# Two of the four sums of weight blocks per unit of seven products, formed by accumulating DMA transfers in place of VectorE additions

## The chip, the cores and the metric

One Trainium2 chip, one of its cores. The engines are TensorE (PE, matrix products), VectorE (DVE), ScalarE (ACT), GpSimd (POOL) and SyncE (SP, which here only issues DMA transfers); PEld are TensorE's weight loads. The metric is the device time of one execution in microseconds, lower is better. Before the change: median 2028.73 us of 3 runs (2027.09 to 2028.84).

## What is computed

Three blocks one after the other on 512 rows of width 1024, all in float32: a block with three mixers (pooling, stick-breaking attention, attention to a memory) and a gated FFN; a block with a gated recurrence and an FFN; a block with latent attention and an FFN. The change touches the three FFNs. The reference, cut to these:

```python
# first block (D_FF = 2816)
gu = n2 @ w_ffn_in[l]                                   # 1024 x 5632
ff = (jax.nn.silu(gu[..., :D_FF]) * gu[..., D_FF:]) @ w_ffn_out[l]

# second and third block
def _conv_ffn(h, w_up, conv_w, conv_b, w_down):
    u = h @ w_up                                        # 1024 x 5632
    ...
    gate, up = jnp.split(y, 2, axis=-1)                 # y: u after a causal convolution over 3 rows
    return (jax.nn.silu(gate) * up) @ w_down
```

## The kernel before, in words

**Products.** Every float32 operand is split into a high part (a copy rounded by ACT, `split`, line 113) and a low part (VectorE subtracts the copy from the original, line 114). A product is three matmuls: high x high, high x low, low x high (`mm3`, lines 107 to 110).

**The FFN.** `ffn` (line 935) goes over the 22 column blocks of 128 in steps of two (line 1007). The first step is done by another routine (`projA_first`). In the ten others, the gate half of the weights is a *unit of seven products*, `seven` (line 304). In the first FFN (`conv is None`) the up half is a unit too, so it has 20 units; the other two FFNs have 10 each, and their up half is an ordinary projection (`projA`, 48 matmuls over 512 columns, with two weight loads of 512 KB). There are 40 units in the program.

**A unit** forms 256 output columns by a scheme of the Strassen kind, with seven half-size products where the ordinary way has eight. The weights of two column blocks, A[0] and A[1], each come as one raw tile of 1024 x 128 (512 KB); each is seen as two halves, A[i][0] and A[i][1] (256 KB each, 128 partitions x 4 runs of 128 numbers). Four sums of these quarter blocks are formed on VectorE (`usum`, lines 324 to 328):

- u1 = A[1][0] + A[1][1], line 333, into a tile of its own (tag "u", two copies)
- u3 = A[0][0] + A[1][0], line 335, in place of A[1][0]
- u2 = u3 + A[1][1], line 336, into a second tile of tag "u"
- u4 = u2 + A[0][1], line 349, in place of u2

The seven products, in order, take as weights A[0][0], u1, u2, A[0][1], u3, A[1][1], u4. `product` (line 317) splits the weights into a tile of tag "w" (eight copies, so that splits can run ahead of TensorE) and issues 12 matmuls over 256 columns. They accumulate in three areas of two PSUM banks: pY, pX, pZ. pX holds the second product, is read by VectorE's subtraction (line 344, which calls line 68), and only then may the seventh product be added to it.

The sums of the activations that the units need (nT1, T3, nT2, T4) are formed once for each FFN by `x_sums` (line 281), on VectorE, in the profile the rows FT<-FT and xc<-FT.

**Buffers and queues.** A[0]'s raw tile lies in the pool wp, A[1]'s in the FFN's own pool; each has two copies. All loads are issued by SyncE (`load`, line 76), in order; a load waits until the last reader of the tile copy that it overwrites is done. The last reader of A[1] is the split of the sixth product (A[1][1]). `seven` is a generator: between its `yield`s, the caller interleaves the units, so that the first product of a unit comes ahead of products six and seven of the one before:

```python
g7 = gate7(f)
next(g7)          # loads, first product
run(tail)         # products 6 and 7 of the unit before
next(g7)          # products 2 to 5
```

**The order of instructions** on each engine is not that of the text: the framework's scheduler orders them by its own estimate of when each is ready, and places semaphores for what depends on what. An engine executes its instructions in that order.

GpSimd executes the powers of the norms (`rstd_of`, line 125), ahead of each FFN's units, and issues no DMA.

**Names in the profile.** Buffer numbers are left out, and the output tile of an up unit of the first FFN is also called u. u1 and u2 are both "u<-raw" (u3 lies in A[1]'s raw tile); u3 is "raw<-raw,raw"; u4 is "u<-u,raw"; the low part of a split is "wu<-raw,wu" or "wu<-u,wu" on DVE, its high part "wu<-raw" or "wu<-u" on ACT.

Of the kernel before, what the change touches and what calls it, by code (L numbers as in the profile page):

```python
# [10 lines left out]
F32 = mybir.dt.float32  # L11
# [4 lines left out]
ALU = mybir.AluOpType  # L16
# [3 lines left out]
P = 128  # L20
# [14 lines left out]
def kernel(ctx: ExitStack, tc: tile.TileContext, a: dict, out: bass.AP):  # L35
    nc = tc.nc
    uid = [0]

    def nm(s):
        uid[0] += 1  # L40
        return f"{s}_{uid[0]}"
# [11 lines left out]
    def bank(s, tag="pj"):  # L53

        return ps.tile([P, 512], F32, tag=tag, name=nm(s), bufs=4 if tag == "pj" else 1)
# [5 lines left out]
    def act(out_, in_, func, **kw):  # L61
        return nc.scalar.activation(out=out_, in_=in_, func=func, **kw)  # L62

    def tt(out_, in0, in1, op):
        return nc.vector.tensor_tensor(out=out_, in0=in0, in1=in1, op=op)  # L65

    def stt(out_, in0, scalar, in1, op0, op1):
        return nc.vector.scalar_tensor_tensor(
            out=out_, in0=in0, scalar=scalar, in1=in1, op0=op0, op1=op1
        )  # L70
# [5 lines left out]
    def load(dst, src):  # L76
        return nc.sync.dma_start(out=dst, in_=src)
# [29 lines left out]
    def mm3(out_, sta, mov, first, last, **kw):  # L107
        nc.tensor.matmul(out_, lhsT=sta[0], rhs=mov[0], start=first, stop=False, **kw)  # L108
        nc.tensor.matmul(out_, lhsT=sta[0], rhs=mov[1], start=False, stop=False, **kw)  # L109
        nc.tensor.matmul(out_, lhsT=sta[1], rhs=mov[0], start=False, stop=last, **kw)  # L110

    def split(src, hi, lo):
        act(hi, src, AF.Copy)
        tt(lo, src, hi.bitcast(F32), ALU.subtract)
# [189 lines left out]
    def seven(w, col, ops, xp, dst, c21, done):  # L304

        A = []
        for i in range(2):
            raw = (wp, xp)[i].tile([P, KD, P], F32, tag="raw", name=nm("raw"), bufs=2)  # L310
            load(raw, w[:, col + i * P : col + (i + 1) * P].rearrange("(k p) n -> p k n", p=P))
            A.append([raw.rearrange("p (c j) n -> p j c n", j=2)[:, j] for j in range(2)])
        bY, bXZ = bank("Y"), bank("XZ")
        pY, pX, pZ = bY[:, :256], bXZ[:, :256], bXZ[:, 256:]
        lf, rt = slice(0, 256), slice(256, 512)

        def product(o, src, key, first):
            t_ = wp.tile([P, 2, 4, P], F32R, tag="w", name=nm("wu"))
            split(src, t_[:, 0], t_[:, 1])
            x_ = ops[key]  # L320
            for c in range(4):
                mm3(o, (t_[:, 0, c], t_[:, 1, c]), (x_[0][:, c], x_[1][:, c]), first and c == 0, c == 3, skip_group_check=True)

        def usum(a_, b_, o=None):
            if o is None:
                o = xp.tile([P, 4, P], F32, tag="u", name=nm("u"), bufs=2)
            tt(o, a_, b_, ALU.add)
            return o

        product(pY, A[0][0], (0, 0), True)  # L330
        act(dst[0][:, lf], pY, AF.Copy)
        yield 1
        u1 = usum(A[1][0], A[1][1])
        product(pX, u1, "nT1", True)
        u3 = usum(A[0][0], A[1][0], A[1][0])
        u2 = usum(u3, A[1][1])
        product(pY, u2, "nT2", False)
        act(dst[0][:, rt], pY, AF.Copy)
        product(pZ, A[0][1], (1, 0), False)
        tt(dst[0][:, lf], pZ, dst[0][:, lf], ALU.add)  # L340
        done(0, 0)
        product(pY, u3, "T3", False)
        act(dst[1][:, rt], pY, AF.Copy)
        stt(dst[1][:, rt], pX, -1.0, dst[1][:, rt], ALU.mult, ALU.subtract)
        done(1, 1)
        yield 1
        product(pY, A[1][1], "T4", False)
        c21(dst[1][:, lf], pY)
        product(pX, usum(u2, A[0][1], u2), (1, 1), False)
        tt(dst[0][:, rt], pX, dst[0][:, rt], ALU.add)  # L350
        done(0, 1)
# [583 lines left out]
    def ffn(w_up, w_down, X, steps, xpool, conv, gpost, gnext, nxt, side="left"):  # L935
        FT = ff["FT"]
        with tc.tile_pool(name=nm("fx"), bufs=1, reuse_waits="tile", side=side) as E:
# [29 lines left out]
            def gate7(f):  # L967

                if conv is None:
                    dst = [FT[:, f], FT[:, f + 1]]  # L970

                    def c21(o, src):
                        act(o, src, AF.Silu, scale=-1.0)

                    def done(q, l):
                        if (q, l) == (1, 1):
                            act(dst[1][:, rt], dst[1][:, rt], AF.Silu)
                        elif (q, l) == (0, 1):
                            act(dst[0], dst[0], AF.Silu)
                else:  # L980
                    dst = [row("g7"), row("g7")]

                    def c21(o, src):
                        act(o, src, AF.Copy, scale=-1.0)
                        gate(f, 1, dst[1])

                    def done(q, l):
                        if (q, l) == (0, 1):
                            gate(f, 0, dst[0])
                return seven(w_up, f * P, ops, E, dst, c21, done)  # L990

            def up7(f):
                dst = [row("u7"), row("u7")]

                def c21(o, src):
                    stt(FT[:, f + 1, lf], src, -1.0, FT[:, f + 1, lf], ALU.mult, ALU.mult)

                def done(q, l):
                    if (q, l) == (1, 1):
                        tt(FT[:, f + 1, rt], FT[:, f + 1, rt], dst[1][:, rt], ALU.mult)  # L1000
                    elif (q, l) == (0, 1):
                        tt(FT[:, f], FT[:, f], dst[0], ALU.mult)
                return seven(w_up, DFF + f * P, ops, E, dst, c21, done)
# [484 lines left out]
```

## Time and profile before

| | |
|---|---|
| time, median of 3 runs | 2028.73 us |
| the profiled execution's own time | 2036.45 us |
| its span | 2034.6 us |
| PE / DVE / ACT / POOL busy | 1990.5 / 1277.1 / 958.0 / 56.4 us |
| DMA | 183.44 MB, 90 GB/s in the mean |
| first FFN's units | about 446 to 657 us of the span |
| second FFN's, third FFN's | about 1110 to 1320 us, 1690 to 1900 us |

The page gives for each engine its busy time, share of the span and number of instructions. The views used below are: a table of stretches (busy time of each engine between two moments); a list of waits (who waited for whom, in total us, times, the longest); the instructions of one tile (smallest/median/largest ns, and what ended the engine's idle time ahead of them); the timeline (start us, duration, engine, line, operation, out<-in; in brackets the idle time ahead of it and what ended it); the chain of work that ended last.

### The profile page before, as it was taken

The page shows a single profiled execution, that of the slowest core. Times are in us where ns is not written, and L with a number is a line of the kernel's source. Part 1 is how long each engine was busy: PE and PEld are TensorE (multiplying, and loading weights), DVE is VectorE, ACT ScalarE, POOL GpSimd, SP SyncE. Part 2 cuts the span into 40 slices and gives each one's busy share as a digit, 9 for nine tenths or more (in the row PEclk, how much of TensorE's full clock was granted, in tenths as well). Part 3 has the DMA queues.
Part 4 walks back from the last instruction along what each step waited for, and adds up shares of the span by engine and source line. Part 5 has one row for each costly group of instructions (what it writes and reads, how often), then busy time and mean ns, then how long its engine had stood idle before and what let it go on. Part 6 is the DMA issues. An engine that isn't in the chain of part 4 may idle for free.

```text
span 2034.6 us, 29719 instructions
## 1 busy us (share of the span) xinstructions
PE 1990.5 (98%) x11665; PEld 1701.7 (84%) x11665; DVE 1277.1 (63%) x2293; ACT 958.0 (47%) x1862; POOL 56.4 (3%) x84
## 2 busy tenths in 40 slices
PE   8999999999999999999999999999989999999999
PEld 6877778889999888888888888888887778888887
DVE  5664543489888336666556887853555558887632
ACT  5543452365555227333244555542357545555521
POOL 0000000000000000000010000000021000000000
PEclk9999999999999999999999999999989999999999
DMA  6332224324333332222213233332230113333322
GB/s 223 90 92 73 69 77 124 104 84 125 102 106 105 93 93 84 73 63 72 70 46 89 83 113 96 93 105 93 66 96 32 42 48 106 96 104 94 104 93 83
DMA packets 192482, 183.44 MB, mean 90 GB/s; under 512 B 6999, under 2 KB 159830, under 8 KB 192342
## 3 DMA queue, kind: packets, MB, share of 16 engines
q1 hardware_dynamic: 192342, 181.54, 29.6%
q8 instruction: 92, 1.51, 0.3%
q14 instruction: 48, 0.39, 0.1%
HBM read 179.42 MB, written 2.10 MB: 89 GB/s over the span
## 4 chain that ended last, share of the span: by engine, by line
PE 80%; DVE 9%; DMA 5%; ACT 3%; issue 2%; POOL 1%; SPq 0%; DVEq 0%; POOLq 0%; ACTq 0%
PE B L108 10%; PE B L110 10%; PE B L109 10%; PE A L108 9%; PE A L109 9%; PE A L110 8%; PE hs L1099 2%; DVE wu L65 2%; PE Y L108 2%; PE Y L109 2%; PE Y L110 2%; DMA raw<-in_w_ffn_in_dram 2%; PE XZ L108 2%; PE XZ L109 2%; PE XZ L110 2%
## 5 line engine op out<-in xcount | busy, mean ns | idle before, releaser
L65 DVE TENSOR_TENSOR wlo<-raw,whi 128x1024 fp32r<-128x1024 f32 (+2 forms) x217 | 257.2, 1187 | 343.7 <-ACT whi L62 343.3
L62 ACT ACTIVATE whi<-raw 128x1024 fp32r<-128x1024 f32 (+2 forms) x217 | 223.9, 1033 | 376.5 <-PE B L109 256.5
L108 PE MATMUL A<-XH,whi 128*128 128x512 f32 (+1 forms) x912 | 337.1, 370 | 0.2 <-ACT XH L62 0.2
L109 PE MATMUL A<-XL,whi 128*128 128x512 f32 (+1 forms) x912 | 332.4, 365 | 0.8 <-DVE XL L65 0.8
L110 PE MATMUL A<-XH,wlo 128*128 128x512 f32 (+1 forms) x912 | 331.7, 364 | 0.0
L110 PE MATMUL B<-whi,yc 128*128 128x512 f32 x528 | 208.0, 395 | 0.0
L108 PE MATMUL B<-whi,yc 128*128 128x512 f32 x528 | 207.6, 393 | 0.0
L109 PE MATMUL B<-wlo,yc 128*128 128x512 f32 x528 | 207.3, 393 | 0.0
L110 PEld LDWEIGHTS A<-XH,wlo 128*128 128x128 f32 x912 | 173.1, 190 | 29.5 <-issue 0.2
L109 PEld LDWEIGHTS A<-XL,whi 128*128 128x128 f32 x912 | 173.3, 190 | 26.4 <-DVE XL L65 1.2
L108 PEld LDWEIGHTS A<-XH,whi 128*128 128x128 f32 x912 | 172.8, 190 | 26.8 <-ACT XH L62 0.7
L108 PE MATMUL B<-whi,XH 128*128 128x512 f32 (+2 forms) x416 | 166.8, 402 | 1.3 <-ACT whi L62 1.3
L109 PE MATMUL B<-wlo,XH 128*128 128x512 f32 (+2 forms) x416 | 158.7, 382 | 1.0 <-DVE wlo L65 1.0
L110 PE MATMUL B<-whi,XL 128*128 128x512 f32 (+2 forms) x416 | 158.7, 383 | 0.0
L108 PE MATMUL Y<-xc,wu 128*128 128x256 f32 x480 | 133.8, 279 | 5.0 <-ACT g L62 3.2
L110 PE MATMUL Y<-xc,wu 128*128 128x256 f32 x480 | 133.0, 277 | 0.0
L109 PE MATMUL Y<-xc,wu 128*128 128x256 f32 x480 | 132.9, 277 | 0.0
L62 ACT ACTIVATE wu<-raw 128x512 fp32r<-128x512 f32 x160 | 98.8, 624 | 46.2 <-DMA raw<-in_ffn_w_up_dram 34.9
L62 ACT ACTIVATE wu<-u 128x512 fp32r<-128x512 f32 x120 | 74.4, 629 | 96.8 <-PE A L109 59.8
L109 PEld LDWEIGHTS B<-wlo,yc 128*128 128x128 f32 x528 | 99.3, 188 | 22.7
L110 PEld LDWEIGHTS B<-whi,yc 128*128 128x128 f32 x528 | 99.4, 188 | 21.8
L108 PEld LDWEIGHTS B<-whi,yc 128*128 128x128 f32 x528 | 99.4, 188 | 21.8 <-issue 0.4
(325 smaller groups left out, 4201.0 us busy)
## 6 DMA issues: line engine op xcount, KB each, us to landing
raw<-in_ffn_w_up_dram SPq DMA_DIRECT2D x88, 512.0 KB
raw<-in_w_ffn_in_dram SPq DMA_DIRECT2D x44, 512.0 KB
raw<-in_ffn_w_down_dram SPq DMA_DIRECT2D x44, 512.0 KB
raw<-in_w_in_dram SPq DMA_DIRECT2D x42, 512.0 KB
raw<-in_hgrn_w_in_dram SPq DMA_DIRECT2D x32, 512.0 KB
raw<-in_w_ffn_out_dram SPq DMA_DIRECT2D x22, 512.0 KB
raw<-in_w_out_dram SPq DMA_DIRECT2D x8, 512.0 KB
raw<-in_hgrn_w_out_dram SPq DMA_DIRECT2D x8, 512.0 KB
```

Source lines behind the costliest of these rows:

```text
L62: return nc.scalar.activation(out=out_, in_=in_, func=func, **kw)
L65: return nc.vector.tensor_tensor(out=out_, in0=in0, in1=in1, op=op)
L108: nc.tensor.matmul(out_, lhsT=sta[0], rhs=mov[0], start=first, stop=False, **kw)
L109: nc.tensor.matmul(out_, lhsT=sta[0], rhs=mov[1], start=False, stop=False, **kw)
L110: nc.tensor.matmul(out_, lhsT=sta[1], rhs=mov[0], start=False, stop=last, **kw)
L1099: nc.tensor.matmul(b[:, sl], lhsT=K[:, e, sl], rhs=Q[:, e, sl], start=True, stop=True)
```

## The change

u1 and u3 are no longer added on VectorE. For u1, SyncE loads A[1][0] a second time, into a tile of its own (tag "u1", two copies; it takes the place of tag "u"), and a DMA transfer issued by GpSimd adds A[1][1] to it from DRAM. For u3, a second transfer issued by GpSimd adds A[0][0] from DRAM to A[1][0] in the raw tile. u2 is written in place of u1, u4 in place of u2 as before.

```diff
             A.append([raw.rearrange("p (c j) n -> p j c n", j=2)[:, j] for j in range(2)])
+        u1 = xp.tile([P, 4, P], F32, tag="u1", name=nm("u1"), bufs=2)
+        blk = [[w[:, col + i * P : col + (i + 1) * P].rearrange("(c j p) n -> p j c n", j=2, p=P)[:, j] for j in range(2)] for i in range(2)]
+        load(u1, blk[1][0])
+        nc.gpsimd.dma_start(out=u1, in_=blk[1][1], accum_op=ALU.add)
+        u3 = A[1][0]
+        nc.gpsimd.dma_start(out=u3, in_=blk[0][0], accum_op=ALU.add)
         bY, bXZ = bank("Y"), bank("XZ")
...
-        def usum(a_, b_, o=None):
-            if o is None:
-                o = xp.tile([P, 4, P], F32, tag="u", name=nm("u"), bufs=2)
+        def usum(a_, b_, o):
             tt(o, a_, b_, ALU.add)
             return o
...
-        u1 = usum(A[1][0], A[1][1])
         product(pX, u1, "nT1", True)
-        u3 = usum(A[0][0], A[1][0], A[1][0])
-        u2 = usum(u3, A[1][1])
+        u2 = usum(u3, A[1][1], u1)
         product(pY, u2, "nT2", False)
```

## Rows read from the trace of the kernel before

**Rows 1.** Page, part 1: busy us (share of the span) x instructions

```profile
PE 1990.5 (98%) x11665; PEld 1701.7 (84%) x11665; DVE 1277.1 (63%) x2293; ACT 958.0 (47%) x1862; POOL 56.4 (3%) x84
```

**Rows 2.** Table of stretches: length, busy us by engine, granted clock, DMA share, GB/s

```profile
457.00:646.00 189.00, 183.16 (x1582) 180.89 (x1582) 167.81 (x325) 109.44 (x222) 0.00 (x0) 1.00 0.37 107
1200.00:1320.00 120.00, 120.00 (x756) 107.01 (x755) 98.09 (x149) 67.14 (x111) 0.00 (x0) 1.00 0.32 94
1120.00:1140.00 20.00, 17.13 (x134) 16.18 (x134) 19.93 (x28) 12.52 (x20) 0.00 (x0) 1.00 0.09 28
1695.00:1705.00 10.00, 6.29 (x51) 5.92 (x50) 10.00 (x16) 7.73 (x13) 0.00 (x0) 0.97 0.17 55
1703.00:1709.00 6.00, 5.88 (x37) 5.88 (x38) 5.05 (x8) 2.44 (x5) 0.00 (x0) 0.72 0.42 134
```

**Rows 3.** List of waits, PE, 430 to 660 us: total us, times, longest

```profile
PE XZ L108 <- DVE u L68: 2.3, 5, 0.7
PE XZ L108 <- DVE FT L68: 2.1, 2, 1.9
```

**Rows 4.** Instructions of tile u on DVE, 457 to 646 us

```profile
L65 DVE TENSOR_TENSOR u<-raw x38: 676/688/696, 459.4 to 637.0; 128x512 f32<-128x512 f32 x38
...
L68 DVE SCALAR_TENSOR_TENSOR u<-XZ,u x9: 411/416/420, 472.6 to 633.9; 128x256 f32<-128x256 f32 x9
...
  DMA raw<-in_w_ffn_in_dram: 13.2, 12
```

**Rows 5.** Timeline, DVE, first FFN

```profile
526.20 0.69 DVE L65 TENSOR_TENSOR wu<-raw,wu 128x512 fp32r<-128x512 f32 x1 [0.74 <-ACT wu L62]
526.99 0.69 DVE L65 TENSOR_TENSOR wu<-u,wu 128x512 fp32r<-128x512 f32 x1
...
530.88 0.69 DVE L65 TENSOR_TENSOR u<-raw 128x512 f32<-128x512 f32 x1 [1.66 <-DMA raw<-in_w_ffn_in_dram]
531.49 0.69 DVE L65 TENSOR_TENSOR wu<-u,wu 128x512 fp32r<-128x512 f32 x1
...
538.82 0.68 DVE L65 TENSOR_TENSOR wu<-u,wu 128x512 fp32r<-128x512 f32 x1
```

**Rows 6.** Timeline, ACT, first FFN

```profile
537.04 0.63 ACT L62 ACTIVATE wu<-u 128x512 fp32r<-128x512 f32 x1 [1.74 <-PE XZ L110]
```

**Rows 7.** Timeline, PE, first FFN: first matmuls of a unit's products two, five and seven

```profile
526.26 0.28 PE L108 MATMUL XZ<-xc,wu 128*128 128x256 f32 x1
...
530.35 0.28 PE L108 MATMUL Y<-xc,wu 128*128 128x256 f32 x1
...
535.30 0.38 PE L108 MATMUL XZ<-XH,wu 128*128 128x256 f32 x1 [0.71 <-DVE u L68]
```

**Rows 8.** Chain of work that ended last: start us, us, what (ten units apart)

```profile
526.91 3.87 DMA raw<-in_w_ffn_in_dram
...
626.09 3.80 DMA raw<-in_w_ffn_in_dram
```

**Rows 9.** Timeline, DVE, start of the second FFN

```profile
1115.79 0.69 DVE L65 TENSOR_TENSOR raw<-raw,raw 128x512 f32<-128x512 f32 x1 [2.16 <-DMA raw<-in_ffn_w_up_dram]
1116.40 2.35 DVE L65 TENSOR_TENSOR FT<-FT 128x1024 f32<-128x1024 f32 x2
```

**Rows 10.** Timeline, ACT, start of the second FFN

```profile
1113.07 1.20 ACT L62 ACTIVATE FT<-tr 128x512 f32<-128x512 f32 x2 [1.52 <-DVE XL L65]
```

**Rows 11.** Timeline, DVE, start of the third FFN

```profile
1684.92 0.69 DVE L65 TENSOR_TENSOR raw<-raw,raw 128x512 f32<-128x512 f32 x1 [1.26 <-DMA raw<-in_ffn_w_up_dram]
```

**Rows 12.** Timeline, SP, ACT, PE, second FFN: load, first split, first matmul

```profile
1278.06 1.59 SPq L77 DMA_DIRECT2D raw<-in_ffn_w_up_dram  x2
...
1283.68 0.63 ACT L62 ACTIVATE wu<-raw 128x512 fp32r<-128x512 f32 x1 [2.69 <-DMA raw<-in_ffn_w_up_dram]
...
1297.04 0.28 PE L108 MATMUL Y<-XH,wu 128*128 128x256 f32 x1
```

**Rows 13.** DMA queues, 541 to 646 us: packets, MB, share of 16 engines

```profile
q1 hardware_dynamic: 19264, 10.49, 34.0%
```

## The prediction

> **What bounds the kernel now.** Read the page's busy times first: TensorE is busy 98% of the span, VectorE 63%, GpSimd 3% [rows 1]. So at most some 2% can be gained anywhere, and only where TensorE waits. The next view is the table of stretches [rows 2]. The change touches the 40 units of seven products: 20 in the first FFN (span 457 to 646 us), 10 in each of the other two. In the first FFN TensorE is busy 183.16 of 189 us, so 5.84 us are open. In the middle of the second it is busy 120.00 of 120: nothing is open there. At the starts of the second and third FFN 2.87 and 3.71 us are open, and VectorE is busy 19.93 of 20 and 10.00 of 10 us: there VectorE sets the pace.
>
> What ends TensorE's waits in the first FFN is in the list of waits: 2.3 and 2.1 us end on VectorE's subtraction at line 68, the one that frees pX for the seventh product [rows 3]. Why that comes late is in the rows of tile u: VectorE stood idle 13.2 us in 12 waits ahead of these sums until a weight load landed [rows 4]. The framework's scheduler has placed the sum u1 far ahead of its use. In the timeline the split of A[1][1] (526.20 us, 0.69 long) frees the second raw buffer, the load into it starts at 526.91 and takes 3.87 us, and u1 of the unit after next starts at 530.88, after 1.66 us of idleness [rows 5, 8]. Its consumer, the ACT copy, runs only at 537.04 [rows 6]. VectorE executes in order, so everything behind u1 waits too, and TensorE loses 0.71 us at 535.30 [rows 7].
>
> **The change, part by part.** (1) Removed from VectorE: u1 and u3, two instructions of 0.69 us per unit [rows 4], 80 in all. They start about 0.61 us apart when back to back [rows 5], so 1.2 us per unit and 49 us in all leave VectorE; almost all of that is off the path. What counts is which TensorE waits they caused.
>
> First FFN: the waits at u1 go with u1. I take away the two groups that end on line 68: 2.3 + 2.1 = 4.4 us [rows 3]. The bounds: 0, if another wait takes the place; at best TensorE's own pace. 36 matmuls start between 526.26 and 530.35, 0.1136 us each [rows 7]; two units have 168, so 19.1 us, against 19.84 us between second-buffer loads two units apart, (626.09 - 526.91) / 5 [rows 8]. That is 0.74 us per pair, 6.7 us over nine pairs.
>
> Starts of the other two FFNs: here u3 (raw<-raw,raw) waits 2.16 and 1.26 us for a load, and the sums of the activations (FT<-FT) stand right behind it, starting at 1116.40 although ACT's copies that they need ran from 1113.07 for 1.20 us [rows 9 to 11]. From there VectorE is busy without a break up to TensorE's gaps. With u3 gone I take 2.2 + 1.3 = 3.5 us, less than the 2.87 and 3.71 us that TensorE idles there [rows 2]. u3's own 0.6 us I don't count, because u2 loses its early place: it now overwrites u1 and so follows the split of u1, with one ACT copy more in series.
>
> Middle of the second and third FFN: 0. TensorE has no gap [rows 2]. The cover is the lead of the splits: ACT's copy for a first product starts at 1283.68 and that product runs at 1297.04, 13.4 us later [rows 12]. Later sums would eat from that first.
>
> (2) Added on SyncE: one 256 KB load per unit, queued behind the two raw loads and ahead of the next unit's. It waits until the seventh split of the unit two before has read the buffer: 526.99 + 0.69 = 527.68, 0.8 us after the second raw load is issued [rows 5, 8]. What stands behind it on SyncE are loads that wait for later releases, so the wait costs nothing by itself.
>
> (3) Added on GpSimd's queue: two accumulating transfers per unit. No row has one. GpSimd runs no instruction in these stretches [rows 2], so their waits hold up only each other; the norm's power steps ahead of the first unit are the exception, with one transfer each at three starts as the bound, and 0 taken. The nearest row for the price is a plain 512 KB load, 3.87 us [rows 8]. Bounds for one: half of it, 1.9 us (256 KB), and two of it, 7.7 us (both operands read, slowly). I take 3.9 us for the first, which reads as many bytes as that load, and 1.9 more for the second, whose landing can overlap: nothing orders the two.
>
> Does that hide? The second raw load and the u1 load land by 526.91 + 3.9 + 1.9 = 532.7; the first accumulation by 536.6. The ACT copy of u1 runs at 537.04 [rows 6]: just in time. u3 is there at 538.5; u2 cannot start before the split of u1 on VectorE at 538.82 is over [rows 5]. Being a little late is covered too: the seventh split of a unit is done at 527.68 and TensorE starts on that product at 535.30 [rows 5, 7], a lead of 7.6 us.
>
> (4) The DMA engines. In the first FFN the load queue takes 34.0% of their time [rows 13] for 1 MB per unit; 0.75 MB are added, 1.25 MB with the destination read. So 60 to 77%: no bound on the mean, but bursts meet (second rival).
>
> The Trainium skill alone has a price for a transfer issued by GpSimd (DMA: Bandwidth & Descriptors, section Anatomy of one DMA — SWDGE (gpsimd) path): a fit of 2.0 us plus size over 436 GB/s, an estimate of 2.6 us for 256 KB, by which the sum would be the same with more room; no run here shows it.
>
> **Sum:** -4.4 - 2.2 - 1.3 = -7.9 us. Durations are of the profiled execution (2036.45 us, span 2034.6), which is 7.7 us above the median of 2028.73; I carry the difference over: 2020.8, so 2021 us.
>
> **Rivals.** *The accumulations bound the first FFN (slower).* The second raw buffer has two copies, so two unit times must hold one cycle: both loads 5.8 us, both accumulations, then u2 to the sixth split. That last part is five splits, u2 and u4 at 0.6 each, two short instructions at 0.4 [rows 4] and one ACT copy at 0.6 [rows 6]: 5.6 us. TensorE needs 19.1, so the accumulations may take 7.7 us together, 3.9 each if they run strictly one behind the other; from there VectorE waits in every unit, at u2 or at the split of u1. At one and a half loads each, 11.6 us, the cycle is 23.0, a unit 11.5 instead of 9.92, over 18 units +28.4, less 3.5 at the starts: 2028.7 + 24.9, 2054 us. For it: each transfer is 512 separate runs of 512 bytes, issued by an engine for which no row has a price, and two come per unit. Against: GpSimd is idle, and the lead is 7.6 us. At 7.7 us each it would be some 2088.
>
> *A wait for a wait (no change).* With the accumulations in flight the loads themselves get slower. Where three loads meet, in the second FFN, the first one, issued at 1278.06, lets ACT start at 1283.68 [rows 12]: 5.6 us in place of 3.87, a factor of 1.45. Then the two loads of the cycle take 8.4 us, the cycle 8.4 + 5.8 + 5.6 = 19.8, a unit 9.9: what it takes now. VectorE and ACT, in order, stand at u2 or at the copy of u1 as long as they stood at u1, and only the starts gain: 2028.7 - 3.5 = 2025.2. For it: my margin at 537.04 is 0.4 us, and it would be gone. Against: the lead of 7.6 us. The Trainium skill has the rule behind it (DMA: Bandwidth & Descriptors, section Issuing engines are not separate DMA queues): transfers started from GpSimd run on the same 16 engines as SyncE's and interleave with them. The trace agrees as far as loads of one queue slow each other; two queues no row shows.
>
> *The clock helps.* At 1703 to 1709, after the gap of the third FFN's start, the granted clock is 0.72 in the mean [rows 2], so part of the stretch ran at the lower level, 1.2 GHz; if that gap shrinks and the clock stays, 6 x 0.28 = 1.7 us more. This belongs to the forecast's low end: -6.7 - 3.5 - 1.7 gives 2016.8.
>
> **How the numbers follow.** Hidden, 2021 us: 0.42. A wait for a wait, 2025: 0.20. Bound by the accumulations, 2054: 0.38; its price is the one that no row gives, and twice my value (11.6 us for my 5.8) gets there. A measurement of this kernel can tell about 0.2%, 4.1 us. So faster 0.42, the same 0.20, slower 0.38. The range reaches from the low end, 2016.5, to 2054: past it lie the worse half of the slow case, some 0.15, and little below. The forecast's own range is 2016.5 to 2024.5.
>
> **What would show it.** Right: between 457 and 646 us TensorE idles under 2 us, VectorE's rows u<-raw fall from 38 to about 19 and stand no longer behind a raw load; the activation sums at the two starts come 1 to 2 us earlier; a unit pair takes 19.1 to 19.3 us. Wrong: ACT's copy of u1 or VectorE's u2 shows waits on DMA of several us in every unit of the first FFN, GpSimd's queue is filled by its two transfers per unit, and a pair takes over 20 us; or the middle of the second FFN shows TensorE waiting, which no step of mine allows.

## The result, and the profile after

The changed kernel takes 2061.38 us (2054.93 to 2065.47), the kernel before 2028.76 on the same chip: a ratio of 1.0153, 95% interval 1.0136 to 1.0170. It is slower, and outside the range. The profiled execution took 2054.93 us, 18.5 more than that of before; it is the shortest of the four, and that of before lies above its median, so the two profiles show less of the loss than the medians, 32.6 us.

Where the time went, by the starts of two kinds of products on TensorE, the third product of the stage's first unit and the seventh of its last (us from the span's start):

| | before | after | change since the line above |
|---|---|---|---|
| first FFN, first unit's third product | 456.2 | 457.8 | +1.6 |
| first FFN, last seventh product | 655.4 | 685.7 | +28.7 |
| second FFN, first unit's third product | 1132.7 | 1159.5 | -3.5 |
| second FFN, last seventh product | 1332.5 | 1360.0 | +0.7 |
| third FFN, first unit's third product | 1703.1 | 1721.9 | -8.7 |
| third FFN, last seventh product | 1903.4 | 1922.2 | 0.0 |

The loss is in the first FFN and nowhere else. Most of the -8.7 is not the change's: the granted clock from 1480 to 1640 us was 0.96 in the execution of before and 0.99 in the same stage of this one. Against the profile of the control e14 below, a kernel as fast as that of before whose clock in this stretch is 0.99 too, the last column reads +2.0, +31.4, -3.6, +1.2, -3.0, +1.6.

The page of the changed kernel, busy times and DMA queues (packets, MB, share of 16 engines); the first line answers to [rows 1]:

```profile
PE 1993.5 (97%) x11665; PEld 1706.9 (83%) x11665; DVE 1238.3 (60%) x2213; ACT 955.6 (47%) x1862; POOL 159.0 (8%) x164
...
q1 hardware_dynamic: 213462, 192.03, 31.5%
q0 software_dynamic: 42240, 20.98, 8.3%
```

VectorE lost its 80 sums, as predicted (2293 instructions to 2213). The new queue carries the 80 accumulations: 8.3% of 2053 us over 80 is 2.1 us of all 16 DMA engines for each.

The table of stretches, columns as in [rows 2]; the first line is the same stretch as there:

```profile
457.00:646.00 189.00, 168.74 (x1368) 166.70 (x1367) 131.79 (x248) 91.79 (x189) 41.49 (x32) 0.95 0.80 163
554.00:558.00 4.00, 0.96 (x8) 0.77 (x7) 2.34 (x4) 2.28 (x5) 1.67 (x2) 0.98 0.11 30
558.00:562.00 4.00, 4.00 (x24) 4.00 (x24) 3.08 (x6) 1.63 (x5) 0.92 (x1) 0.60 1.05 136
```

TensorE now idles 20 us of the 189 where it idled 5.84, and VectorE is no longer near its limit. After a gap such as that from 554 to 558 us the granted clock falls (0.60 in the next 4 us, so most of them at 1.2 GHz): a stall costs more than its own length.

What waits, in the list of waits of this stretch (us in total, times, longest):

```profile
ACT wu L62 <- DMA u<-in_w_ffn_in_dram: 40.2, 13, 5.9
...
PE Y L108 <- ACT u L62: 10.2, 4, 5.5
PE Y L108 <- ACT FT L62: 10.1, 6, 3.0
```

The waits that end on VectorE's line 68 [rows 3] are gone. In their place ACT's copy of u1 stands 40.2 us for the accumulation, and TensorE waits for what ACT does behind it, the freeing of bank Y. The DMA view gives the accumulations' median times from issue to landing in the first FFN:

```profile
raw<-in_w_ffn_in_dram POOLq DMA_DIRECT2D x20, 256.0 KB, 4.6
u<-in_w_ffn_in_dram POOLq DMA_DIRECT2D x20, 256.0 KB, 6.9
```

Those of u1 lie between 6.5 and 8.5 us. Some expectations below reckon with 8.3, from the slow ones on the chain of work.

The timeline follows one of u1's two copies round:

```profile
539.96 0.37 SPq L77 DMA_DIRECT2D u<-in_w_ffn_in_dram  x1
...
544.74 1.28 POOL L318 DMA_DIRECT2D raw<-in_w_ffn_in_dram  x1 [8.75 <-DMA raw<-in_w_ffn_in_dram]
545.54 1.79 POOL L316 DMA_DIRECT2D u<-in_w_ffn_in_dram  x1
...
554.15 0.63 ACT L62 ACTIVATE wu<-u 128x512 fp32r<-128x512 f32 x1 [4.61 <-DMA u<-in_w_ffn_in_dram]
...
564.24 0.69 DVE L65 TENSOR_TENSOR wu<-u,wu 128x512 fp32r<-128x512 f32 x1 [0.67 <-ACT wu L62]
...
564.96 0.37 SPq L77 DMA_DIRECT2D u<-in_w_ffn_in_dram  x1
```

It is loaded at 539.96. The accumulation into it is issued 5.6 us later: the scheduler has put u3's accumulation first on GpSimd, and that one waited until 544.74 for the second raw load. It lands 8.5 us after its issue, and ACT has waited 4.61 us for it. The copy then holds u1, u2 and u4 until the seventh split ends at 564.93, 10.8 us on, and the next load goes at once. The round takes 25.0 us here, the longest of them (the shortest takes 21.2), and two units can't go faster than one round. Over the whole first FFN it is (685.7 - 457.8) / 10 = 22.8 us for two units, against TensorE's 19.1.

### The profile page after: what moved, and what is told of

Read it like the earlier page. It is cut to its first block, busy times and chain, and to the rows that moved or that the text cites. A ratio compares the mean times of both kernels' runs of the same rounds, so it can differ in the third digit from the quotient of the medians.

```text
span 2053.1 us, 29904 instructions
## 1 busy us (share of the span) xinstructions
PE 1993.5 (97%) x11665; PEld 1706.9 (83%) x11665; DVE 1238.3 (60%) x2213; ACT 955.6 (47%) x1862; POOL 159.0 (8%) x164
## 3 DMA queue, kind: packets, MB, share of 16 engines
q0 software_dynamic: 42240, 20.98, 8.3%
## 4 chain that ended last, share of the span: by engine, by line
PE 79%; DMA 8%; DVE 7%; ACT 3%; issue 2%; POOL 1%; SPq 0%; ACTq 0%; POOLq 0%; DVEq 0%
PE B L108 10%; PE B L109 10%; PE B L110 10%; PE A L108 9%; PE A L109 9%; PE A L110 9%; DMA u<-in_w_ffn_in_dram 4%; PE hs L1101 2%; PE Y L108 2%; PE Y L109 2%; PE Y L110 2%; DMA raw<-in_w_ffn_in_dram 1%; DVE wu L65 1%; PE XZ L108 1%; PE XZ L110 1%
## 5 line engine op out<-in xcount | busy, mean ns | idle before, releaser
L108 PE MATMUL Y<-xc,wu 128*128 128x256 f32 x480 | 137.8, 287 | 27.1 <-ACT FT L62 12.9
L65 DVE TENSOR_TENSOR wu<-u,wu 128x512 fp32r<-128x512 f32 x120 | 82.7, 689 | 96.7 <-ACT wu L62 95.8
L125 POOL TENSOR_TENSOR r<-v,mhalf 128x1 f32<-128x1 f32 (+2 forms) x62 | 43.0, 695 | 1202.3 <-DVE v L74 1197.7
L110 PE MATMUL Y<-xc,wu 128*128 128x256 f32 x480 | 135.7, 283 | 0.0
L109 PE MATMUL Y<-xc,wu 128*128 128x256 f32 x480 | 135.5, 282 | 0.0
L65 DVE TENSOR_TENSOR wu<-raw,wu 128x512 fp32r<-128x512 f32 x160 | 108.5, 687 | 34.1 <-ACT wu L62 33.7
```

The costliest lines, as they stand in the source:

```text
L125: nc.gpsimd.tensor_tensor(out=r, in0=v, in1=mhalf[:, :w], op=ALU.pow)
```

## The experiments

Two theories at first. *Holding time*: with two copies, load, accumulations and sums don't fit into two units; more copies or a shorter hold would mend it. *Traffic*: the DMA engines themselves are the bound. Ratios are to the kernel before on the same chip.

### Where, how many copies, which accumulation

```diff
# e1: the change in the second and third FFN alone
+        if dma:        # conv is not None
             u1 = xp.tile(...)
# e2: more copies (and the split of T4 left out)
-  tag="u1", name=nm("u1"), bufs=2          tag="raw", ... bufs=2)
+  tag="u1", name=nm("u1"), bufs=4          tag="raw", ... bufs=2 + i)
# e3
-        nc.gpsimd.dma_start(out=u1, in_=blk[1][1], accum_op=ALU.add)
+        usum(u1, A[1][1], u1)
# e4
-        nc.gpsimd.dma_start(out=u3, in_=blk[0][0], accum_op=ALU.add)
+        usum(A[0][0], u3, u3)
```

> The change is made in the second and third FFN alone; the first FFN forms its sums as before. Both theories put the whole loss of about 29 us in the first FFN and a gain of 2.4 to 2.5 us at the start of each later one. So 2028.8 - 5 = 2024 us, a small gain. If it comes out at 2029 or above, the starts' gain is given back later, and the account of the loss by stage is wrong.

Measured: 2028.88 us, 0.9997 (0.9987 to 1.0007): no loss, so all of it is in the first FFN, but no gain of 5 us either. On this the expectation missed; the part on the starts below says why.

> The changed kernel with four copies of tile u1 in place of two and three of the second raw tile in place of two. To make room the split of the activation sum T4 is left out, and the sixth product reads the pieces of T3, so its output is not the reference's; TensorE does as many products as before. Latency (two copies can't hold load, accumulations and sums, some 23 us for two units): the first FFN falls back to 9.6 to 9.9 us a unit, its last product ends near 655 to 658 us, and the time is 2027 to 2033 us. Traffic (the 16 DMA engines are the bound, 8.7 us of transfers per unit that queue behind each other): more copies change nothing, a unit stays at 11.3 to 11.5 us and the time at 2056 to 2063 us.

Measured: 2029.69 us, 1.0003 (0.9989 to 1.0017). The copies bring back all of the loss, while the DMA engines are busier than in the changed kernel (0.83 of their time from 457 to 646 us, against 0.80). Traffic is no bound by itself.

> The change without u1's accumulation: VectorE adds A[1][1] to the loaded copy of A[1][0]; u3 is still formed by an accumulating transfer. Latency: the copy of u1 waits for a load only, u3 lands some 8.5 us after the second raw load is issued (3.9 + 4.6) and is needed after u1's split; the cycle of the second raw buffer is about 3.9 + 4.6 + 5.6 = 14 us, under the 19.1 that TensorE needs, so the first FFN is as fast as before or 4 us faster: 2021 to 2030 us. Traffic: 6.5 us of transfers per unit in place of 8.7 takes away about half of the loss: 2040 to 2050 us.

> The change without u3's accumulation: VectorE forms u3 in place of A[1][0] as before; u1 is still loaded and accumulated. Latency: with nothing ahead of it on GpSimd the accumulation into u1 starts when its load has landed and takes 4.6 to 6 us; cycle 5.8 + 4.6 to 6 + 5.6 to 7 = 16 to 19 us, at or under 19.1, so the first FFN is within 3 us of before; the starts lose their gain: 2027 to 2034 us. Traffic: about half of the loss stays, 2040 to 2050 us. If this one is slow and the kernel without u1's accumulation is not, it is u1's place (third load, then accumulation) that costs, not the number of transfers.

Measured: 2050.43 us, 1.0105 (1.0086 to 1.0124), and 2058.99 us, 1.0150 (1.0127 to 1.0172). Both missed the quick case: without one of the two accumulations most of the loss stays. Something else slows the first FFN as soon as VectorE forms one of these sums again.

### What is dear, what is held, what disturbs

```diff
# e5: u1's copy is freed by u1's split
-        u2 = usum(u3, A[1][1], u1)
+        u2 = usum(u3, A[1][1], A[0][0])
# e6: both accumulations replaced by VectorE's sums (e3 and e4 together)
# e7: the kernel before, and in each unit
+        load(v1, blk[1][0])
+        nc.gpsimd.dma_start(out=v1, in_=blk[1][1], accum_op=ALU.add)
+        nc.gpsimd.dma_start(out=v3, in_=blk[0][0], accum_op=ALU.add)
# e8: both transfers without the addition
-        nc.gpsimd.dma_start(out=u1, in_=blk[1][1], accum_op=ALU.add)
+        nc.gpsimd.dma_start(out=u1, in_=blk[1][1])
```

> The changed kernel with u2 (and u4 after it) put into the place of A[0][0], which is done with by then, in place of u1; all transfers stay as they are. Holding time: u1's copy is now freed by the split of u1 and not by the seventh split. In the changed kernel one copy goes round in 23.3 us for two units: 4.2 us from the load to the accumulation's issue, 8.3 to its landing, 10.8 from there to the next load. The 10.8 would fall to about 1.5, the round to 14 us, under the 19.1 that TensorE needs; the second raw buffer is next, at 17 to 20 us. So the first FFN is back at 9.6 to 10 us a unit: 2022 to 2034 us. If the price of the transfers themselves or the load on the DMA engines bounds the first FFN, nothing changes: 2055 to 2064 us.

Measured: 2045.78 us, 1.0084 (1.0068 to 1.0100). Half comes back, not all, so neither case was met. The list of waits, 457 to 646 us, names what binds next:

```profile
ACT wu L62 <- DMA raw<-in_w_ffn_in_dram: 42.3, 17, 4.1
...
DVE raw L65 <- DMA raw<-in_w_ffn_in_dram: 24.7, 14, 2.3
```

The first raw buffer is now held to the seventh split, so the first product's split waits for its load, and u2 (raw<-raw,raw) waits for u3's accumulation. The hold was only moved.

> No accumulation at all: u1's place is loaded with A[1][0] as a third load, VectorE adds A[1][1] to it and forms u3 as before, and u2 stays in u1's place. The version without u1's accumulation stood at 2050 us with VectorE's first sum behind that load in every unit (5.4 us from issue to the sum, 5.8 from there to the seventh split: 11.2 a unit). If the third load in the round is the cause there, it is slow here too: 2040 to 2050 us. If the accumulation into u3 was, this one is at 2025 to 2031 us.

Measured: 2047.18 us, 1.0095 (1.0079 to 1.0110), without any accumulation. Its chain of work shows why (start, us, what):

```profile
530.74 4.00 DMA raw<-in_w_ffn_in_dram
...
541.83 3.92 DMA u<-in_w_ffn_in_dram
...
551.53 3.85 DMA raw<-in_w_ffn_in_dram
...
562.46 3.69 DMA u<-in_w_ffn_in_dram
```

From 530 us on every unit of some 10.4 us has one whole load on the chain. Where VectorE forms a sum from a freshly loaded block, the scheduler puts that sum ahead of the unit before's last splits; those free the buffer for the next load, and that load is what the next such sum waits for. So a unit is one load and some 6 us, and two copies give no more room than one would. Before, it is 3.87 us and 6 [rows 5, 8]. In e4 the chain has this form from 530 us on too, with loads of 3.9 to 5.4 us. In e3 it passes through a load in some units only, 3.6 to 5.2 us each; there VectorE's first sum waited for its load 15 times between 457 and 646 us, 26.6 us in all. That this alone is e3's loss is not shown.

> The kernel before, with the change's three transfers per unit (one load, two accumulations) into tiles that nothing reads, so they take the DMA engines' and GpSimd's time but nothing waits for them. To make room the split of T4 is left out and the sixth product reads T3's pieces. If the transfers do harm by slowing the loads (3.87 to about 5 us, one load per unit in the round), the first FFN's unit goes from 9.9 to about 11 us: 2040 to 2052 us. If only the waiting for them does harm: 2025 to 2032 us.

Measured: 2132.25 us, 1.0514 (1.0498 to 1.0531), outside both. This run doesn't tell: its third load must wait on SyncE until the accumulation into the same copy has landed, and the raw loads that follow stand behind it there (SyncE waited 76.1 us for it from 457 to 646 us, in 15 waits); VectorE waited up to 15.5 us for one. It was built again without that load, as e9.

> The changed kernel with the two accumulating transfers turned into plain ones of the same bytes, issued by GpSimd in the same places and waited for in the same way; the two additions of weight blocks are left out. If the accumulation is what is dear (8.3 us from issue to landing in the first FFN, 2.1 us of all DMA engines each), a plain transfer lands in 3 to 4 us, the round of u1's copy is 4.2 + 3.5 + 10.8 = 18.5 us, under 19.1, and the time is 2025 to 2036 us. If the chain of two transfers, the issue by GpSimd and the holding time are enough by themselves: 2045 to 2060 us.

Measured: 2027.81 us, 0.9994 (0.9984 to 1.0004). With plain transfers the whole loss is gone. The page's queue and the DMA view, which answer to the two of the changed kernel:

```profile
q0 software_dynamic: 6400, 20.98, 3.5%
```

```profile
raw<-in_w_ffn_in_dram POOLq DMA_DIRECT2D x20, 256.0 KB, 3.5
u<-in_w_ffn_in_dram POOLq DMA_DIRECT2D x20, 256.0 KB, 4.2
```

The same 20.98 MB go in 6400 packets, 80 to a transfer, where the accumulating ones take 42240, 528 to a transfer, one to each run of 512 bytes and 16 more. A plain transfer takes 0.9 us of all DMA engines (3.5% of 2027 us over 80), an accumulating one 2.1.

### The disturbance alone, and what could win

```diff
# e9: the kernel before, and in each unit, for two spare tiles v
+            nc.gpsimd.tensor_copy(out=v[:, 0, 0:1], in_=A[1][1][:, 0, 0:1])
+            nc.gpsimd.dma_start(out=v, in_=src, accum_op=ALU.add)
# e10: e2, and the first two units without the change
# e11: the same with raw's bufs=2, T4's split kept, and yp bufs=4
+        if dma:        # conv is not None or f > 2
# e12: the kernel before
-            raw = (wp, xp)[i].tile(..., bufs=2)        yp = ... bufs=6
+            raw = (wp, xp)[i].tile(..., bufs=2 + i)    yp = ... bufs=4
```

> The kernel before, with two accumulating transfers per unit into four spare tiles that nothing reads, and no third load. GpSimd copies one column of the second raw buffer into a spare tile ahead of each, so that they come once per unit, about when the change's would; SyncE's queue waits for none of them. To make room the split of T4 is left out and the sixth product reads T3's pieces. If the accumulations harm by slowing the weight loads beside them (3.87 us to about 5, one load in the round of each unit of the first FFN): 2040 to 2052 us. If only waiting for an accumulation harms: 2026 to 2032 us.

Measured: 2057.96 us, 1.0167 (1.0137 to 1.0197), past the harmful case. Transfers that nothing reads cost about as much here as the whole change. Its chain of work, which answers to [rows 8]:

```profile
536.93 4.93 DMA raw<-in_w_ffn_in_dram
...
548.04 5.86 DMA raw<-in_w_ffn_in_dram
...
559.78 4.96 DMA raw<-in_w_ffn_in_dram
...
617.17 6.50 DMA raw<-in_w_ffn_in_dram
```

The eleven loads on the chain from 500 to 640 us take 5.33 us in the mean; the ten of before in the same stretch, 3.91. That is 1.4 us a load, one load a unit: 28 us over 20 units.

> The version with four copies of u1 and three of the second raw tile, with the first two units of the first FFN summed by VectorE, so that no accumulation stands on GpSimd ahead of the norm's power steps. To make room the split of T4 is left out and the sixth product reads T3's pieces. The version with more copies had 162.4 us of products in the 164 us from 476 on, against 158.9 before (3.5 us gained), but at the first FFN's start TensorE waited 6.9 us for the norm (2.0 before) and ran some us at the lower clock. If that wait is GpSimd's queue, it falls back to about 2 us and the time is 2021 to 2026 us; if not, it stays at 2027 to 2032.

> The same late start with nothing left out: four copies of u1, but two of the second raw tile; the room comes from the rows' ring y, four in place of six. If u1's copies alone are what bounds the first FFN (23.3 us in the round for two units), this is as fast as the version with both, 2021 to 2027 us, and it beats both kernels. If the second raw buffer is the next to bind (load 5.3, accumulation 4.6 to 6, then to the sixth split, 18 to 21 us for two units) or the shorter ring y holds something up: 2030 to 2045 us.

Measured: 2027.52 us, 0.9997 (0.9985 to 1.0009), and 2028.52 us, 1.0001 (0.9991 to 1.0011). TensorE's wait for the norm did fall to 2.0 us in both, but neither beats before, so both expectations missed. The hidden change is worth nothing measurable. In e10's profile the first FFN, from its first product to its last seventh one, is 5.3 us shorter than the control's (194.1 for 199.4), and the second 7.8 us longer (211.4 for 203.6); why is not shown.

> The kernel before with three copies of the second raw tile in place of two and the ring y cut from six rows to four, no accumulating transfer anywhere. VectorE's first sum then needn't wait for a load (13.2 us of idleness in 12 waits in the first FFN), so the first FFN should gain the 3 to 4 us that the hidden versions gained there, and each later start about 1 to 2 us: 2022 to 2026 us. If the ring y holds up the products' rows, or other waits take their place: 2028 to 2035 us.

Measured: 2018.03 us, 0.9957 (0.9941 to 0.9973). This one beats both kernels, by more than was expected. The stretches from 476 to 640 us, inside the first FFN, of four kernels: before, with three raw copies, of e2, and changed:

```profile
476.00:640.00 164.00, 158.89 (x1373) 156.82 (x1372) 144.99 (x281) 94.51 (x191) 0.00 (x0) 1.00 0.37 107
```

```profile
476.00:640.00 164.00, 164.00 (x1402) 163.90 (x1401) 149.34 (x288) 97.10 (x194) 0.00 (x0) 1.00 0.36 105
```

```profile
476.00:640.00 164.00, 162.36 (x1429) 162.16 (x1430) 134.02 (x245) 98.06 (x199) 40.12 (x31) 1.00 0.89 183
```

```profile
476.00:640.00 164.00, 149.24 (x1200) 147.39 (x1200) 115.19 (x213) 82.07 (x168) 38.90 (x30) 0.95 0.79 159
```

With a third copy of the second raw tile VectorE's sums wait for no load from 457 to 646 us (10.3 us in 10 waits in the control below) and TensorE has no gap left, with all of VectorE's 80 sums still there. They were not too many; they stood behind a load. But a busy TensorE is not always equally fast: in these 164 us it starts 1402 matmuls in this kernel and 1429 in e2, so one takes 117.0 and 113.6 ns, at a granted clock of 1.00 in both. What slows them the runs don't show. In this execution the first FFN is therefore only 0.6 us shorter than the control's (198.8 for 199.4).

### What was still open

```diff
# e13: e9 with e12's edits; e14: e12 without its third raw copy
# e15: the changed kernel
-  tag="u1", name=nm("u1"), bufs=2          yp = ... bufs=6
+  tag="u1", name=nm("u1"), bufs=4          yp = ... bufs=4
# e16: the changed kernel, its first two units without the change
```

> The same two unread accumulations per unit as in the paced run, on the kernel before with three copies of the second raw tile (ring y cut to four rows; the split of T4 left out and the sixth product reads T3's pieces). The paced run came to 2058 us with its weight loads at 4.6 to 6.5 us in place of 3.8 to 4.4. If those slower loads harm only because VectorE's first sum stands right behind a load in every unit, the third copy takes the load out of the round and the time is 2018 to 2030 us. If the accumulations harm in another way too (VectorE or ACT held up beside GpSimd, the clock), it stays at 2040 to 2058 us.

Measured: 2026.39 us, 0.9993 (0.9980 to 1.0007). Once the load is out of the round, the same unread traffic no longer costs 30 us. So most of its harm came from slowing that load. It isn't free even so: the kernel with three raw copies and no traffic stands at 0.9957, some 7 us lower.

> The control: the kernel before with the ring y cut from six rows to four and nothing else. The version with three raw copies stood at 0.9957 of before. If the third copy did that, this one is at 2026 to 2032 us or slower; if the shorter ring did (it changes where the scheduler puts things), it is at 2018 to 2024 us.

Measured: 2027.32 us, 0.9995 (0.9984 to 1.0006): the shorter ring alone gains nothing, so the gain of e12 is the third copy's. In 476 to 640 us this control shows:

```profile
476.00:640.00 164.00, 162.64 (x1397) 161.64 (x1396) 147.51 (x284) 96.67 (x196) 0.00 (x0) 1.00 0.38 110
```

> The changed kernel with four copies of u1 in place of two, two of the second raw tile, ring y at four rows, all units accumulated; nothing left out. If the round of u1's copy (23.3 us for two units) is what bounds the changed kernel's first FFN, this alone brings it back: 2027 to 2036 us, with the norm's wait behind GpSimd's queue still there. If the second raw buffer's accumulation binds as well: 2040 to 2058 us.

Measured: 2033.94 us, 1.0033 (1.0021 to 1.0045). Four copies of u1 (with the shorter ring, which the control shows to do nothing by itself) bring back some 26 of the 33 us. The rest is at the stage's start: the first unit's first product comes at 463.4 us, at 453.1 in the control. GpSimd's timeline there (e15), and then that of the kernel before:

```profile
445.05 1.28 POOL L316 DMA_DIRECT2D u<-in_w_ffn_in_dram  x1 [4.46 <-DMA u<-in_w_ffn_in_dram]
445.82 1.11 POOL L125 TENSOR_TENSOR r<-v,mhalf 128x1 f32<-128x1 f32 x1
```

```profile
438.63 1.00 POOL L125 TENSOR_TENSOR r<-v,mhalf 128x1 f32<-128x1 f32 x1 [7.87 <-DVE rot L74]
```

The norm's last power step comes 7.2 us late, because it stands on GpSimd behind an accumulation that waited 4.46 us for its load. TensorE's list of waits, 420 to 480 us, shows what that costs (2.0 us in e10, 6.9 in e2):

```profile
PE tr L86 <- DVE n L68: 10.3, 2, 8.6
```

> The changed kernel, two copies of each as there, with the first two units of the first FFN summed by VectorE (no third load and no accumulation in them). This moves only the start. Two units less in the round of 23.3 us for two save at most 4 us, and the norm's wait some us more: 2052 to 2060 us. If the start's pile of transfers on GpSimd's queue is what makes the later units late, far more comes back: 2030 to 2045 us.

Measured: 2058.06 us, 1.0149 (1.0133 to 1.0164). With two copies the late start changes nothing; e11, which has both mends, loses nothing.

## Why the prediction was wrong

**The price of the accumulations** is the step that failed first: "I take 3.9 us for the first", "and 1.9 more for the second". Measured, u3's takes 4.6 us and u1's 6.9 from issue to landing, up to 8.5, one behind the other on GpSimd and with u3's ahead. The forecast counted 9.7 us from the issue of the second raw load to the landing of u1 (3.9 + 1.9 + 3.9); in the round above that load is issued at 538.90 and u1 lands at 554.05, 15.1 us later. The forecast had 0.4 us of margin at the copy of u1. Both medians lie inside the bounds given (1.9 to 7.7) and above the 3.9 that was taken, the time of a plain load. The Trainium skill's fit for a GpSimd transfer (DMA: Bandwidth & Descriptors, section Anatomy of one DMA — SWDGE (gpsimd) path), from which the prediction has its estimate of 2.6 us, was further off; even the plain transfers of e8 took 3.5 and 4.2 us in the median.

**The cover** failed with it. The lead of 7.6 us between a split and its product can absorb one delay, but the same delay in every unit adds up.

**The rival "accumulations bound the first FFN"** was what happened, and its size (+28.4 us) came out at 28.7, or 31.4 against the control's profile. Its sum was near by luck: 5.8 for the loads, 11.6 for the accumulations, 5.6 to the sixth split; the trace shows 5.6, 8.5 and 10.8 to the seventh split, 25.0 in place of 23.0, on u1's copy instead of the second raw buffer's. That u2 in u1's place holds that copy so long was seen as one ACT copy more in series, not as a buffer held.

**"A wait for a wait"** was a real mechanism with the wrong host. Accumulations do slow the loads beside them, by 1.36 (5.33 over 3.91 us; the rival had 1.45), and it costs 30 us in e9, where VectorE's sum waits for a load. In the changed kernel VectorE waits for no load from 457 to 646 us, and the slow loads count only as part of u1's round.

**The gain itself** was the other failed step: "-4.4" for TensorE's waits on line 68. The change did remove them. But they belong to the one profiled execution of before, 7.7 us above the median: TensorE was busy 158.89 us of 164 there, 162.64 in the control and 162.72 in e1, whose first FFN is the program of before. About 1.3 us were to be had in those, not 4.4. Part of the difference is TensorE's own pace: a matmul takes 116.4 ns of busy time in the control, 115.7 in before and 113.6 in e2, and a slower TensorE waits less. How much of the 4.4 an average execution had to give is not shown.

**The starts.** From the last product of tile hs at line 1099 of the kernel before, ahead of the second FFN, to the third product of that FFN's first unit it is 109.1 us before and 109.5 in the control, 106.6 with the change and 106.5 in e1: 2.5 to 3.0 us gained, where 2.2 was predicted. From the first product of tile mz to the third FFN's third product it is 181.1 us in the control and 179.6 in e1: 1.5 gained, where 1.3 was predicted. (Up to the unit's first product it is 1.8 to 2.4 and 0.8.) Both terms held in size. But e1's middles, from the third product to the last seventh one, take 1.9 and 1.1 us longer than the control's, where the prediction had 0. By equal numbers of matmuls after tile hs, e1 is ahead of the control by 3.2 us at 118 us and by 1.1 at 143 us, so what the second FFN's start gains is mostly given back within its first units; what holds it up there is not shown. What is left, -1.5 us, lies within the interval of e1.

**The clock.** At the third FFN's start the granted clock was 1.00 with the change (1720 to 1728 us), as the rival hoped, but it was 1.00 in the control too (1693 to 1699 us), so this is not shown to be the change's doing. In the first FFN it fell from 1.00 to 0.95 over the 189 us from 457 to 646: some 9 us of full speed lost, which no rival had.

**Right:** VectorE's rows u<-raw fell by half, to one a unit, the waits on line 68 in the first FFN went, the starts came earlier, and the signs named for "wrong" (ACT's copy of u1 waiting on DMA, a pair over 20 us) were the ones that showed. GpSimd's queue ahead of the norm was named as an exception and put at 0: it cost TensorE 1.1 us more of waiting in the changed kernel (3.1 for 2.0), and 8.3 us in e15.

Left open: why e12's median lies 9 us below the control's when their profiles differ by 3.2. The profile of each is one execution, and executions of one kernel spread over up to 14 us here; e12's profiled one, 2022.71 us, is among its slowest (2017.05 to 2023.38), and has the slow matmuls told of above. So the runs show that the third copy gains time, but not in which stage.

## What to carry to other kernels

Before moving a sum off an engine, ask whether the engine is short of time or only stands behind a load: here one more copy of the loaded buffer gave the time that the change was hoped to give, and without new traffic. A step turned into a transfer lengthens the life of the buffer that it lands in, so count every copy's round (load, transfers, last reader) against the units that it must serve; and look at how far the profiled execution lies above the median before adding up its waits.

## What the runs showed of the hardware

An accumulating 256 KB transfer of 512-byte runs costs 2.4 times the DMA engines' time of a plain one (2.1 and 0.9 us of all 16), goes in 528 packets in place of 80, and is issued more slowly by GpSimd. The lines of GpSimd's instructions, changed kernel and e8 (457 to 690 us; busy us, mean ns):

```profile
L316 POOL DMA_DIRECT2D u<-in_w_ffn_in_dram x18 | 29.2, 1620 | 2.6 <-DVE wu L65 1.9 <-DVE u L65 0.7
```

```profile
L316 POOL DMA_DIRECT2D u<-in_w_ffn_in_dram x18 | 13.5, 750 | 8.0 <-DVE wu L65 3.5 <-DVE FT L65 2.2 <-DVE u L65 0.9
```

The Trainium skill (DMA: Bandwidth & Descriptors, section SWDGE vs HWDGE vs iDMA) gives 4096 bytes as the preferred upper limit of a packet. Both kinds stay under it here, the plain transfers with 3.3 KB and the accumulating ones with about 0.5 KB a packet, so the limit doesn't tell them apart. That the many small packets are what makes them dear fits these numbers but was not tried by itself.
